# A two-layer mixture-of-experts block with attention: a written order for the first part, a late residual bias, loads held for the first gather, and token rows added in DRAM by the DMA

## The chip, the cores and the metric

The kernel runs on one core of one Trainium2 chip, in one launch. The metric is device time in microseconds (us), the median of several runs; lower is better.

## The reference

The model width D is 1024. There are T = 512 latent tokens x and 256 context tokens s. Everything is float32. The kernel computes two blocks; the change touches the first, which has two layers. The second (two more attentions and convolutional feed-forward layers) follows unchanged and is left out here.

```python
for i in range(2):                                  # first block
    sh1, sc1, g1, sh2, sc2, g2 = adaln(c, w_mod[i], b_mod[i])     # silu(c) @ w_mod + b_mod, 6 x D
    a = rmsnorm(x, norm1_g[i]) * (1 + sc1) + sh1
    if i == 0:   y = pool_mixer(a)                  # the same on the context, with its own c
    else:        y = attn_mixer(a, a_ctx)           # 16 query heads, 4 key heads, keys of x and s
    x = x + g1 * y
    x = x + g2 * hier_moe(rmsnorm(x, norm2_g[i]) * (1 + sc2) + sh2)
    # layer 0 does both lines for the context s too; layer 1 only reads it

def pool_mixer(h):                 # 4 groups of 256 channels, windows of 2, 4, 8, 16 tokens
    p = [window_mean(h_g, w) - h_g for g, w in groups]
    return (einsum(p, w_pool) + b_pool) * ls

def hier_moe(h):                   # 16 experts in 4 groups: best group, then top 2 in it
    gates = ...                    # one row of 16 per token, two of them not zero
    a, b = h @ w_gate[e], h @ w_up[e]               # 1024 x 256 for each expert e
    return sum_e (silu(a) * b * gates[e]) @ w_down[e]
```

## The kernel before

**Layout.** Channels lie on partitions in 8 chunks of 128, tokens along the free axis: x is 8 x (128 x 512), the context xc is 8 x (128 x 256). Matrix products with large weights are made from three float32-round products: `split_w` (L285 to 296) casts a weight tile to its high part (L294, ScalarE) and subtracts it for the low part (L295, DVE or GpSimd); `mm3` (L353 to 355) adds the three products. Weights come by `load_raw` (L303 to 320): each load is 512 KB, all are issued on SyncE's queue and keep their written order. Their slots are a ring of 6 tiles of the pool `raw` and two for each larger tile given to `ring`; a load waits until the slot is read out. A load can be given a *hold*: it then waits for a named DMA, and since the queue is in order all later loads wait with it.

**Order.** A planner at build time orders each engine's instructions by priority (written order) and readiness, so written order and engine order differ unless an edge is added by hand (`issue_after`, `add_manual_dep`).

**Layer 0, first part (L1085 to 1155).** w_mod has 12 blocks of 2 MB for each layer, in the order 0, 2, 1, 3, 4, 5, 8, 9, 6, 7, 10, 11. A block is `adaln_mm` (four loads, 16 matmuls at L380, a copy by ScalarE at L385) and `adaln_end` (four transposes, two small DVE operations). In between stand, for the latent rows (r = 0) and the context (r = 1) and four channel groups g: `pool_pre` (normalise, L479 and L481), `pool_win` (window sums by scan, L495 to 507) and `pool_back` (the 256 x 256 group product L521, the residual bias by ScalarE at L518, gate and residual add by DVE at L523). Then the MoE's entry: `moe_chunk` (ScalarE scales a chunk at L587 and squares it at L589; the matmuls of the router and of the sum of squares at L594), `moe_shift` (the shift's part of the logits, and the shift as broadcast rows `b2r`, copied at L615), `moe_close` (evacuation L622, transposes, logits L627, 1/rms with ScalarE's square root L192, L630, L631) and `moe_tr` (transposes of a token block and, on DVE at L648, times 1/rms plus shift; L649 writes the rows to `h2d` in DRAM, by GpSimd's queue in layer 0 and by ScalarE's in layer 1).

**Routing and experts (`moe_run`).** DVE turns the logits into lists of token numbers per expert (to L780). GpSimd gathers an expert's rows from `h2d` with an indirect DMA (L834), 128 rows in layer 0 and 96 in layer 1; TensorE transposes them (`rows_t`), then come gate/up and down products, and ScalarE's queue writes results to `yd` (L899). At the end `fetch` gathers two rows of `yd` for each token. `Stream` issues expert weights (four loads gate/up and two loads down for each expert) some experts ahead. In layer 0 it also carries two blocks of layer 1's w_mod, at the places "a" and "b" ahead of the routing; each of these calls `more(1)` twice, which issues the next expert weights.

**Layer 1** has the latent rows alone: `moe_shift` stands ahead of the output product wo (`gemm_8`), whose chunks call `moe_chunk` as they come; then five tiles are given to the ring, `moe_close`, `moe_tr` and `moe_run` follow.

Of the kernel before, what the change touches and what calls it, by code (L numbers as in the profile page):

```python
# [63 lines left out]
def build(tc, A, out, stop=None, dbg=None):  # L64
# [98 lines left out]
    def vc(name, i=0, n=1):  # L163
        o = _VEC[name] + i
        return vec[:, o : o + n]

# [155 lines left out]
    class Stream:  # L322
# [50 lines left out]
    def adaln_mm(l, nb, st=None, got=None):  # L373
        ps = PS()
        if not st and got is None:
            got = adaln_load(l, nb)
        for u in range(2):
            raw = st.take(("ad", l, nb, u)) if st else got[u]
            for kk in range(4):
                mm(ps[32 * kk : 32 * kk + 32, :], cs[:, 4 * u + kk, :], raw[kk // 2][:, kk % 2 * 512 : kk % 2 * 512 + 512],  # L380
                   start=(u == 0), stop=(u == 1), tile_position=(0, 32 * kk))
            if st:
                st.more(1)
        adps[l, nb] = t2()
        S.copy(adps[l, nb], ps)  # L385
# [126 lines left out]
    def pool_back(r, g):  # L512
        xr, n, _ = rows[r]
        ps_p = pooled.pop((r, g))
        g_, b_ = gl[r, g // 2]
        for f in range(2):
            c = 2 * g + f
# [5 lines left out]
            V.scalar_tensor_tensor(xr[:, c, :], ps[:, :n], g_[:, c % 4 : c % 4 + 1], xr[:, c, :], op0=ALU.mult, op1=ALU.add)  # L523
# [29 lines left out]
    def moe_start(l, segs, cap):  # L553
# [5 lines left out]
        for xr, n, r in segs:  # L559
            q = K()  # L560
            q.xr, q.n, q.r, q.nb, q.tb0, q.psl, q.seen, q.due = xr, n, r, n // 128, st.ntb, None, 0, []
            st.ntb += q.nb
            st.segs.append(q)
# [15 lines left out]
    def moe_chunk(st, i, c):  # L579
# [7 lines left out]
        S.activation(hch(q, c), q.xr[:, c, :], AF.Copy, scale=q.a2[:, c : c + 1])  # L587
        sq = t2()
        S.activation(sq[:, : q.n], q.xr[:, c, :], AF.Square)  # L589
        q.due += [(st.wr[:, c, :], hch(q, c)), (e20, sq[:, : q.n])]  # L590
        if len(q.due) == 4:

            for k, (w, v) in enumerate(q.due):
                mm(q.psl[32 * k : 32 * k + 32, : q.n], w, v, start=q.seen == 0, stop=q.seen == 3, tile_position=(0, 32 * k))  # L594
            q.due = []
            q.seen += 1

    def moe_shift(st, i):
# [11 lines left out]
        q.b2r = half("b2")  # L610
        for h_ in range(2):
            pt = PS()
            for c in range(4):
                transpose(pt[:, c * 128 : c * 128 + 128], b2[:, 4 * h_ + c : 4 * h_ + c + 1].to_broadcast([128, 128]))
            S.copy(q.b2r[:, 512 * h_ : 512 * h_ + 512], pt)  # L615

    def moe_close(st, i):
# [4 lines left out]
        S.copy(ev[:, :n], q.psl[:, :n])  # L622
# [5 lines left out]
        q.rs = rstd_from(lg[:, :, 20], 1.0 / D, [128, nb], f"n2_{q.r}")  # L628
        lg = lg[:, :, 0:20]
# [3 lines left out]
        def tr(b):  # L633
# [10 lines left out]
            def second():  # L644
                ht = half("ht")
                for h_, pt in enumerate(pts):
                    hs_ = slice(512 * h_, 512 * h_ + 512)
                    V.scalar_tensor_tensor(ht[:, hs_], pt, q.rs[:, b : b + 1], q.b2r[:, hs_], op0=ALU.mult, op1=ALU.add)  # L648
                (G if len(st.segs) > 1 else S).dma_start(st.h2d[(q.tb0 + b) * 128 : (q.tb0 + b) * 128 + 128, :], ht)  # L649
# [3 lines left out]
        st.trs += [tr(b) for b in range(nb)]  # L653

# [13 lines left out]
    def moe_run(st, wst):  # L668
# [121 lines left out]

        def late():


            gd = gsm([128, N, 4], tag="gd")
            V.tensor_tensor(gd, gl_, bc(gm.rearrange("p (n o) -> p n o", o=1), [128, N, 4]), op=ALU.subtract)
# [4 lines left out]
            v1, v2 = (gsm([128, N], tag=f"v{j}") for j in range(2))  # L800
            for v_, va in ((v1, v1a), (v2, v2a)):
                V.tensor_tensor(va, va, goh, op=ALU.mult)
                V.reduce_sum(v_, va, axis=AX.X)
            ed = gsm([128, N], tag="ed")
            V.tensor_tensor(ed, v2, v1, op=ALU.subtract)
# [34 lines left out]
        def gather(e):  # L840
            xg[e] = half("xg")
            gather_rows(xg[e][0:cap, :], idx[0:cap, e : e + 1])
# [240 lines left out]


    mst = moe_start(0, rows, 128)  # L1085
    sss = [stats(0)]
    adaln_block(0, 0)
    rb[0] = bcast(sss[0].compact("n1_0"), T)
    adaln_block(0, 2)
    a1[0, 0] = half_cols(0, 0)  # L1090
    pool_pre(0, 0)
    adaln_mm(0, 1)
    pool_win(0, 0)
    pool_pre(0, 1)
    adaln_end(0, 1)
    adaln_mm(0, 3)
    pool_win(0, 1)
    adaln_end(0, 3)
    a1[0, 1] = half_cols(0, 1)
    nc.sync.dma_start(poolw, A["poolw"])  # L1100
    adaln_mm(0, 4)
    pool_pre(0, 2)
    adaln_end(0, 4)
    nc.sync.dma_start(xc, A["ctxT"])
    pool_win(0, 2)
    gl[0, 0] = half_gate(0, 0)
    pool_back(0, 0)
    adaln_mm(0, 5)
    pool_pre(0, 3)
    pool_back(0, 1)  # L1110
    adaln_end(0, 5)
    pool_win(0, 3)
    sss.append(stats(1))
    gl[0, 1] = half_gate(0, 1)
    for h_ in range(2):
        a1[1, h_] = half_cols(1, h_)
        gl[1, h_] = half_gate(1, h_)
    pool_back(0, 2)
    adaln_mm(0, 8)
    rb[1] = bcast(sss[1].compact("n1_1"), TC)  # L1120
    pool_pre(1, 0)
    adaln_end(0, 8)
    pool_back(0, 3)
    pool_win(1, 0)
    adaln_mm(0, 9)
    pool_pre(1, 1)
    adaln_end(0, 9)
    pool_win(1, 1)
    for c in range(4):
        moe_chunk(mst, 0, c)  # L1130
    pool_back(1, 0)
    adaln_mm(0, 6)
    pool_pre(1, 2)
    for c in range(4, 8):
        moe_chunk(mst, 0, c)
    adaln_end(0, 6)
    pool_win(1, 2)
    pool_back(1, 1)
    adaln_mm(0, 7)
    pool_pre(1, 3)  # L1140
    adaln_end(0, 7)
    pool_win(1, 3)
    moe_shift(mst, 0)
    moe_shift(mst, 1)
    pool_back(1, 2)
    moe_close(mst, 0)
    pool_back(1, 3)
    for c in range(4):
        moe_chunk(mst, 1, c)
    moe_tr(mst, 4)  # L1150
    for c in range(4, 8):
        moe_chunk(mst, 1, c)
    adaln_block(0, 10)
    moe_close(mst, 1)
    adaln_block(0, 11)
# [657 lines left out]
    moe_shift(mst, 0)  # L1813
    g1 = shift(1, 2, 0)
# [27 lines left out]
    ring.extend(s8() for _ in range(5))  # L1842
# [676 lines left out]
```

## Time and profile before

| | |
|---|---|
| time, median of 3 runs (lowest, highest) | 2222.83 us (2222.02, 2226.96) |
| the profiled execution: its own time, its span | 2218.79 us, 2217.0 us |
| mean granted TensorE clock, share of full speed | 0.973 |
| busy: PE, DVE, ACT, POOL | 93%, 64%, 50%, 23% |
| moved by DMA | 323.43 MB, mean 146 GB/s |

PE is TensorE, DVE VectorE, ACT ScalarE, POOL GpSimd and SP SyncE. PEld is TensorE's weight load; a name with q (SPq, ACTq) is an engine's issuing of DMAs. Times in the rows are from the start of the span. The first part of layer 0 and its MoE lie at 0 to 316 us, layer 1's at 316 to 873 us.

### The profile page before, as it was taken

Reading aid. Unit: us, or ns where it says so; the run is one execution under the profiler, and the core shown is the slowest. Engines: PE = TensorE matmul, PEld = TensorE weight load, DVE = VectorE, ACT = ScalarE, POOL = GpSimd, SP = SyncE. Lnnn points to the kernel's source line nnn. Section 1 sums busy time; section 2 is a strip of 40 time slices with the busy share of each in tenths; the row PEclk is TensorE's granted clock in tenths of the full one; section 3 lists DMA queues with packets and bytes.
Section 4 is the critical chain, followed back from the end, with each engine's and each line's share of the span. In section 5 each row is a group of like instructions: output and inputs, shape, how many; then the busy total and the mean of one; then the engine's idle time right before and its main releaser. Section 6 shows DMA issues by size and latency. Waiting matters only on the chain.

```text
span 2217.0 us, 32294 instructions
## 1 busy us (share of the span) xinstructions
PE 2067.5 (93%) x12233; PEld 1683.7 (76%) x12233; DVE 1418.8 (64%) x2304; ACT 1102.1 (50%) x1967; POOL 509.6 (23%) x513
## 2 busy tenths in 40 slices
PE   6869998999994999999999999999999999999997
PEld 1348767788863767776698888999878888888997
DVE  4579878778726987367847666626363568565633
ACT  3648864488833886344434434324253455343422
POOL 1011021477201212245423101014100024101011
PEclk9889999999997999999999999999999999999998
DMA  9699973124606996321113333332322212333321
GB/s 376 260 351 398 417 282 101 50 77 137 217 21 219 369 391 211 99 77 48 58 52 102 94 100 91 98 93 68 97 86 86 67 48 89 101 96 96 96 77 39
DMA packets 94207, 323.43 MB, mean 146 GB/s; under 512 B 11537, under 2 KB 17184, under 8 KB 93536
## 3 DMA queue, kind: packets, MB, share of 16 engines
q1 hardware_dynamic: 76480, 274.76, 36.0%
q0 software_dynamic: 7968, 28.32, 3.6%
q10 hardware_dynamic: 9600, 18.26, 2.2%
q8 instruction: 97, 1.59, 0.3%
q14 instruction: 62, 0.51, 0.1%
HBM read 301.02 MB, written 20.27 MB: 145 GB/s over the span
## 4 chain that ended last, share of the span: by engine, by line
PE 65%; DVE 7%; DMA 4%; POOL 3%; ACT 3%; issue 3%; ACTq 0%; DVEq 0%; POOLq 0%; SPq 0%
PE ps L353 19%; PE ps L355 18%; PE ps L354 18%; PE ps L177 3%; DMA s<-in_mgu_dram 1%; PE ps L1722 1%; DVE lo L295 1%; POOL raw L1762 1%; PE ps L2103 1%; PE ps L2254 1%; DVE s L1939 1%; ACT hi L294 1%; DMA raw<-in_mdn_dram 1%; PE ps L2059 1%; DVE s L1931 1%
## 5 line engine op out<-in xcount | busy, mean ns | idle before, releaser
L353 PE MATMUL ps<-s,hi 128*128 128x512 f32 (+1 forms) x1440 | 513.5, 358 | 4.3 <-DVE s L1931 3.2
L354 PE MATMUL ps<-s,hi 128*128 128x512 f32 (+1 forms) x1440 | 505.6, 351 | 3.0 <-DVE s L1939 1.8
L355 PE MATMUL ps<-s,lo 128*128 128x512 f32 (+1 forms) x1440 | 507.4, 353 | 0.0
L294 ACT CAST hi<-raw 128x1024 fp32r<-128x1024 f32 x284 | 294.0, 1047 | 419.2 <-PE ps L354 334.2
L295 DVE TENSOR_TENSOR lo<-raw,hi 128x1024 fp32r<-128x1024 f32 x232 | 288.2, 1256 | 277.5 <-ACT hi L294 277.3
L295 POOL TENSOR_TENSOR lo<-raw,hi 128x1024 fp32r<-128x1024 f32 x52 | 125.4, 2411 | 892.1 <-ACT hi L294 892.1
L353 PEld LDWEIGHTS ps<-s,hi 128*128 128x128 f32 x1440 | 270.5, 188 | 45.7 <-issue 8.0
L354 PEld LDWEIGHTS ps<-s,hi 128*128 128x128 f32 x1440 | 271.3, 188 | 41.4 <-DVE s L1939 2.4
L355 PEld LDWEIGHTS ps<-s,lo 128*128 128x128 f32 x1440 | 271.1, 188 | 41.1 <-issue 0.5
L353 PE MATMUL ps<-hi,s 128*128 128x512 f32 (+1 forms) x528 | 216.8, 412 | 4.6 <-ACT hi L294 2.0
L354 PE MATMUL ps<-lo,s 128*128 128x512 f32 (+1 forms) x528 | 211.9, 401 | 2.6 <-DVE lo L295 2.6
L355 PE MATMUL ps<-hi,s 128*128 128x512 f32 (+1 forms) x528 | 211.3, 401 | 2.5 <-DVE s L1839 2.5
L355 PE MATMUL ps<-t2r,lo 128*128 128x256 f32 (+1 forms) x640 | 188.2, 294 | 0.0
L354 PE MATMUL ps<-t2r,hi 128*128 128x256 f32 (+1 forms) x640 | 187.8, 293 | 0.0
L353 PE MATMUL ps<-t2r,hi 128*128 128x256 f32 (+1 forms) x640 | 187.8, 293 | 0.0
L353 PEld LDWEIGHTS ps<-hi,s 128*128 128x128 f32 (+1 forms) x528 | 105.3, 199 | 30.1 <-ACT hi L294 4.4
L355 PEld LDWEIGHTS ps<-hi,s 128*128 128x128 f32 (+1 forms) x528 | 105.2, 199 | 29.0 <-DVE s L1839 4.1
L354 PEld LDWEIGHTS ps<-lo,s 128*128 128x128 f32 (+1 forms) x528 | 105.9, 201 | 25.7 <-DVE lo L295 3.1
L353 PEld LDWEIGHTS ps<-t2r,hi 128*128 128x128 f32 x640 | 121.2, 189 | 5.2 <-issue 2.5
L354 PEld LDWEIGHTS ps<-t2r,hi 128*128 128x128 f32 x640 | 121.1, 189 | 5.3 <-issue 2.5
L355 PEld LDWEIGHTS ps<-t2r,lo 128*128 128x128 f32 x640 | 120.8, 189 | 5.2 <-issue 2.5
L295 DVE TENSOR_TENSOR lo<-s,hi 128x1024 fp32r<-128x1024 f32 x98 | 114.8, 1217 | 5.2 <-ACT hi L294 4.7
(371 smaller groups left out, 3667.2 us busy)
## 6 DMA issues: line engine op xcount, KB each, us to landing
raw<-in_up_dram SPq DMA_DIRECT2D x88, 512.0 KB
s<-in_mgu_dram SPq DMA_DIRECT2D x64, 512.0 KB
raw<-in_mgu_dram SPq DMA_DIRECT2D x44, 512.0 KB
raw<-in_down_dram SPq DMA_DIRECT2D x44, 512.0 KB
raw<-in_dilqkv_dram SPq DMA_DIRECT2D x36, 512.0 KB
s<-in_mdn_dram SPq DMA_DIRECT2D x34, 512.0 KB
raw<-in_wmodT_dram SPq DMA_DIRECT2D x32, 512.0 KB
s<-in_wmod_dram SPq DMA_DIRECT2D x30, 512.0 KB
```

Source lines behind the costliest of these rows:

```text
L177: return PE.transpose(dst, src, ident if idt is None else idt)
L294: S.copy(hi, raw)
L295: eng.tensor_tensor(lo, raw, hi, op=ALU.subtract)
L353: mm(ps, ahi, bhi, start=start, stop=False)
L354: mm(ps, ahi, blo, start=False, stop=False)
L355: return mm(ps, alo, bhi, start=False, stop=stop)
L1722: mm(po_[c][o : o + 64, qb * 128 : qb * 128 + 128], vview[:, kc, c // 2 * 64 : c // 2 * 64 + 64], PTs[h_][:, kc * 128 : kc * 128 + 128], s ...
L1762: G.tensor_tensor(w, w, crow, op=ALU.mult)
L1931: V.tensor_tensor(mv, mv, bc(self.rb[:, None, 0:256], [128, 2, 256]), op=ALU.mult)
L1939: V.scalar_tensor_tensor(self.h.lo(c)[:, ts], x[:, c, ts], g_, self.h.hi(c)[:, ts], op0=ALU.mult, op1=ALU.subtract)
L2059: mm(pz[:, o : o + n], qq, kk, start=True, stop=True)
L2103: mm(po[64 * hh : 64 * hh + 64, kb * 128 : 512], vt, at[:, o : o + n], start=(kb == 0), stop=(kb == 3), tile_position=(0, 64 * hh))
```

## The change

- **A written order.** `in_order` links the instructions of TensorE, ScalarE and DVE in the whole first part, each to the one before it on its engine, so that they run as written. The part is written anew: the first four blocks' loads ahead, each later block's loads after the matmuls of an earlier one; `pool_back` is cut into `back_mm` and `back_add`; context squares are summed by matmuls (`sum_stats`); context chunks alternate with the `moe_tr` of one token block; blocks 10 and 11 come after everything else.
- **The bias late.** The 16 operations at L518 leave `pool_back`. `moe_chunk` takes the bias into its scale and its square; `back_bias` adds it to the residual after the last `moe_close`.
- **Loads held.** The places "a" and "b" no longer issue expert loads. These 8 loads follow the first gather in layer 0, and are held until it has landed. Six small DVE operations of the gate weights are moved ahead of the first weight splits.
- **Layer 1's rows.** The shift rows are written to `h2d` by ScalarE's queue well ahead. `moe_tr` then needs only a scaled copy by ScalarE in place of L648, and GpSimd's queue issues a DMA that adds the rows to those in DRAM. The square-root table is loaded right after the evacuation, and the ring gets its five tiles ahead of wo.

```diff
+    @contextlib.contextmanager
+    def in_order():
+        cur = nc.cur_bb.bb.instructions
+        known = {id(i) for i in cur}
+        yield
+        prev = {}
+        for i in cur:
+            if id(i) in known or i.engine not in (V.engine, S.engine, PE.engine):
+                continue
+            if i.engine in prev:
+                tc.add_manual_dep(i, prev[i.engine].name, mybir.DependencyInfo(
+                    mybir.DependencyClass.NoSync, mybir.DependencyReason.DATA), reason="in order")
+            prev[i.engine] = i
...
-                adaln_mm(*b, self)
+                adaln_mm(*b, self, more=k not in ("a", "b"))
...
-            S.activation(xr[:, c, :], xr[:, c, :], AF.Identity, bias=b_[:, c % 4 : c % 4 + 1])
...
+    def back_bias(r):
+        xr, n, _ = rows[r]
+        for c in range(NCH):
+            S.activation(xr[:, c, :], xr[:, c, :], AF.Identity, bias=gl[r, c // 4][1][:, c % 4 : c % 4 + 1])
...
+            S.activation(hch(q, c), q.xr[:, c, :], AF.Identity, scale=q.a2[:, c : c + 1], bias=q.a2b[:, c : c + 1])
+            S.activation(sq[:, : q.n], q.xr[:, c, :], AF.Square, bias=bias[c // 4][:, c % 4 : c % 4 + 1])
...
+        evac = S.copy(ev[:, :n], q.psl[:, :n])
+        if len(st.segs) == 1:
+            sqrt_table(evac)
...
+                    if q.there:
+                        st.s_last = S.activation(ht[:, hs_], pt, AF.Copy, scale=q.rs[:, b : b + 1])
+                    else:
+                        V.scalar_tensor_tensor(ht[:, hs_], pt, q.rs[:, b : b + 1], q.b2r[:, hs_], op0=ALU.mult, op1=ALU.add)
+                if q.there:
+                    G.dma_start(to, ht, accum_op=ALU.add)
+                else:
+                    G.dma_start(to, ht)
...
+            for b in range(q.nb):
+                S.dma_start(st.h2d[(q.tb0 + b) * 128 : (q.tb0 + b) * 128 + 128, :], q.b2r)
...
-        for e in range(3):
+        first = gather(0)
+        with tc.issue_after(gated.ins):
+            firsts = late_first()
+        if wst.ads:
+            hold[:] = [first]
+            wst.more(2 * sum(len(v) for v in wst.ads.values()))
+        for e in range(1, 3):
             gather(e)
         wst.side("c")
         if not wgu:
-            with tc.issue_after(gated.ins):
+            with tc.issue_after(firsts.ins), tc.issue_after(st.s_last.ins):
                 moe_weights(st, wst, 0, V)
...
+        ad(5, 7)
...
+        ad(8, 10)
...
+        ad(9, 11)
+        back_add(1, 0)
+        chunks(0, 0)
+        pool_win(1, 3)
+        back_add(1, 1)
+        back_mm(1, 2)
+        ad(6)
+        chunks(0, 1)
+        back_mm(1, 3)
+        back_add(1, 2)
+        ad(7)
+        back_add(1, 3)
+        moe_shift(mst, 0)
+        moe_shift(mst, 1)
+        chunks(0, 2)
+        moe_shift_rows(mst, 0)
+        chunks(0, 3)
+        moe_close(mst, 0)
+        chunks(1, 0)
+        moe_tr(mst, 1)
...
+        chunks(1, 3)
+        moe_tr(mst, 1)
+        moe_close(mst, 1)
+        moe_shift_rows(mst, 1)
+        for r in range(2):
+            back_bias(r)
+    ad(10)
+    ad(11)
...
+    moe_shift_rows(mst, 0, there=True)
+    ring.extend(s8() for _ in range(5))
...
-    ring.extend(s8() for _ in range(5))
```

## Rows read from the trace of the kernel before

**Rows 1.** Windows: busy time of each engine in seven stretches.
```profile
40.00:97.00 57.00, 49.72 (x206) 17.57 (x202) 31.79 (x76) 28.55 (x57) 2.96 (x15) 0.90 0.86 336
97.00:118.00 21.00, 16.45 (x125) 12.91 (x124) 12.77 (x32) 10.69 (x27) 2.38 (x4) 0.84 0.38 143
137.00:146.00 9.00, 0.61 (x3) 0.64 (x4) 5.19 (x13) 0.00 (x0) 5.60 (x4) 0.50 1.03 416
180.00:283.00 103.00, 101.34 (x486) 82.36 (x485) 93.55 (x108) 89.50 (x128) 11.30 (x10) 1.00 1.02 415
620.00:670.00 50.00, 49.39 (x190) 30.57 (x189) 10.24 (x13) 15.29 (x23) 2.40 (x1) 1.00 0.04 11
690.00:700.00 10.00, 1.78 (x16) 1.58 (x16) 5.81 (x13) 0.25 (x1) 5.51 (x4) 0.50 1.03 380
785.00:825.00 40.00, 37.69 (x184) 26.30 (x184) 34.40 (x41) 32.97 (x50) 9.19 (x4) 1.00 1.03 389
```

**Rows 2.** Timeline of ACT, 90 to 122 us: start, duration, idle before and releaser.
```profile
95.87 0.59 ACT L385 COPY t<-ps 128x512 f32<-128x512 f32 x1 [2.95 <-PE ps L380]
...
117.02 0.58 ACT L385 COPY t<-ps 128x512 f32<-128x512 f32 x1 [5.94 <-PE ps L380]
117.50 0.38 ACT L622 COPY t<-ps 128x256 f32<-128x256 f32 x1
```

**Rows 3.** Timeline of DVE, 100 to 124 us: the last operation on the logits.
```profile
120.36 0.20 DVE L631 TENSOR_TENSOR g<-g,g 128x40 f32<-128x40 f32 x1
```

**Rows 4.** Groups by line and shape, 0 to 137 us: busy, mean ns, idle before.
```profile
L518 ACT ACTIVATE x<-x,sm 128x512 f32<-128x512 f32 x8 | 5.2, 711 | 4.3 <-DVE sm L450 4.3
L518 ACT ACTIVATE xc<-xc,sm 128x256 f32<-128x256 f32 x8 | 3.8, 495 | 0.0
```

**Rows 5.** Waits of SP's queue, 50 to 160 us: in total, times, longest.
```profile
SPq L314 <- PE ps L380: 47.9, 11, 19.8
```

**Rows 6.** Timeline, 134 to 150 us: the first gathers of layer 0.
```profile
136.72 0.16 DVE L780 CAST g<-ps 128x14 int32<-128x14 f32 x1
136.80 4.62 DVE L295 TENSOR_TENSOR lo<-raw,hi 128x1024 fp32r<-128x1024 f32 x4
137.09 1.82 POOL L834 DMA_INDIRECT s<-h2d,g  x1 [10.35 <-DVE g L780]
...
141.43 0.94 POOL L834 DMA_INDIRECT s<-h2d,g  x1 [0.30 <-issue]
...
145.39 1.94 PE L177 MATMUL ps<-ident,s 128*128 128x128 f32 x8 [8.81 <-DMA s<-h2d,g]
```

**Rows 7.** Timeline, 296 to 320 us: the last gathers of the latent rows in layer 0.
```profile
307.00 1.87 POOL L834 DMA_INDIRECT s<-yd,g  x1 [0.30 <-issue]
...
313.63 1.29 DVE L930 SCALAR_TENSOR_TENSOR s<-s,g 128x1024 f32<-128x1024 f32 x1 [1.77 <-DMA s<-yd,g]
313.65 3.19 SPq L314 DMA_DIRECT2D raw<-in_wmod_dram  x6
```

**Rows 8.** Waits of TensorE, 165 to 300 us.
```profile
PE ps L353 <- ACT hi L294: 1.6, 3, 0.7
```

**Rows 9.** Timeline, 670 to 706 us: layer 1 from its last logits to its first rows.
```profile
673.40 1.28 ACT L192 ACT_TABLE_LOAD   x1
...
676.07 0.75 DVE L648 SCALAR_TENSOR_TENSOR s<-ps,sm,s 128x512 f32<-128x512 f32 x1
...
691.48 1.78 POOL L834 DMA_INDIRECT s<-h2d,g  x1 [53.51 <-DVE g L780]
...
698.84 1.51 PE L177 MATMUL ps<-ident,s 96*128 96x96 f32 x8 [7.85 <-DMA s<-h2d,g]
```

**Rows 10.** Groups by line and shape, 670 to 700 us.
```profile
L648 DVE SCALAR_TENSOR_TENSOR s<-ps,sm,s 128x512 f32<-128x512 f32 x8 | 5.8, 740 | 0.0
```

**Rows 11.** The chain that ended last, 600 to 720 us: start, duration, what.
```profile
678.97 2.67 DMA h2d<-s
...
693.57 10.53 DMA s<-h2d,g
```

**Rows 12.** Waits of SP's queue, 590 to 700 us.
```profile
SPq L314 <- DMA h2d<-s: 55.2, 4, 48.8
```

More of the change, by code (lines that the diff above doesn't have):

```diff
@@ L371, in adaln_load, with adaln_mm @@
         return [load_raw(A["wmod"][l, nb, :, 2048 * u : 2048 * u + 2048]) for u in range(2)]
-    def adaln_mm(l, nb, st=None, got=None):
+    def adaln_mm(l, nb, st=None, got=None, more=True):
         ps = PS()
@@ L381, in adaln_mm @@
                    start=(u == 0), stop=(u == 1), tile_position=(0, 32 * kk))
-            if st:
+            if st and more:
                 st.more(1)
@@ L560, in moe_start @@
             q = K()
[L561 removed]
+            q.xr, q.n, q.r, q.nb, q.tb0, q.psl, q.seen, q.due, q.there = xr, n, r, n // 128, st.ntb, None, 0, [], False
             st.ntb += q.nb
@@ L577, in hch, with moe_chunk @@
         return q.hts[c // per][:, (c % per) * q.n : (c % per) * q.n + q.n]
-    def moe_chunk(st, i, c):
+    def moe_chunk(st, i, c, bias=None):
         q = st.segs[i]
@@ L609, in moe_shift @@
         V.tensor_tensor(q.cst[:, 0, :], pc[:, 0:20], rbias[:, st.l, :], op=ALU.add)
[L610 to L615, printed above, removed]
     def moe_close(st, i):
@@ L1104, in build @@
[L1104 to L1155, printed above, removed]
+    got = {}
+    def ad_load(nb):
+        got[nb] = adaln_load(0, nb)
+    def ad(nb, nxt=None):
+        adaln_mm(0, nb, got=got.pop(nb))
+        if nxt is not None:
+            ad_load(nxt)
+        adaln_end(0, nb)
+    def chunks(i, j):
+        for c in (2 * j, 2 * j + 1):
+            moe_chunk(mst, i, c, bias=[gl[i, h_][1] for h_ in range(2)])
@@ new lines, in build @@
+    mst = moe_start(0, rows, 128)
+    with in_order():
+        for nb in (0, 2, 1, 3):
+            ad_load(nb)
+        nc.sync.dma_start(poolw, A["poolw"])
+        ss0 = stats(0)
+        ad(0, 4)
+        nc.sync.dma_start(xc, A["ctxT"])
+        rb[0] = bcast(ss0.compact("n1_0"), T)
+        ad(2, 5)
+        a1[0, 0] = half_cols(0, 0)
+        pool_pre(0, 0)
+        pool_pre(0, 1)
+        pool_win(0, 0)
+        pool_win(0, 1)
+        ad(1, 8)
+        ad(3, 9)
+        a1[0, 1] = half_cols(0, 1)
+        pool_pre(0, 2)
+        back_mm(0, 0)
+        pool_pre(0, 3)
+        pool_win(0, 2)
+        ad(4, 6)
+        gl[0, 0] = half_gate(0, 0)
+        back_mm(0, 1)
+        for h_ in range(2):
+            a1[1, h_] = half_cols(1, h_)
+        ss1 = sum_stats(1)
+        pool_win(0, 3)
+        back_add(0, 0)
+        back_add(0, 1)
+        rb[1] = bcast(rstd_from(ss1, 1.0 / D, [128, 2], "n1_1"), TC)
+        pool_pre(1, 0)
+        ad(5, 7)
+        gl[0, 1] = half_gate(0, 1)
+        for h_ in range(2):
+            gl[1, h_] = half_gate(1, h_)
+        back_mm(0, 2)
+        back_mm(0, 3)
+        pool_pre(1, 1)
+        pool_win(1, 0)
+        back_add(0, 2)
+        back_add(0, 3)
+        pool_pre(1, 2)
+        pool_win(1, 1)
+        ad(8, 10)
+        back_mm(1, 0)
+        pool_pre(1, 3)
+        back_mm(1, 1)
+        pool_win(1, 2)
+        ad(9, 11)
[18 more added lines that the diff above has]
+        moe_tr(mst, 1)
+        chunks(1, 1)
+        moe_tr(mst, 1)
+        chunks(1, 2)
+        moe_tr(mst, 1)
+        chunks(1, 3)
+        moe_tr(mst, 1)
+        moe_close(mst, 1)
+        moe_shift_rows(mst, 1)
+        for r in range(2):
+            back_bias(r)
```

92 lines of the change are left out of this document (54 added, 38 removed).

## The prediction, made before the changed kernel was run

> **What bounds the kernel now.** I read the windows first, then the timelines at their borders, then the waits and the chain. The windows [rows 1] show that the two layers are made of stretches with different limits. In the experts of layer 0 (180 to 283 us) PE is busy 101.34 of 103 us while the DMA engines are full too (1.02): the two are in balance, and PE waited for data only 1.6 us between 165 and 300 us [rows 8]. In layer 1's experts the DMA engines are full again and PE loses 2.3 of 40 us. What is not full lies ahead of the experts. In 40 to 118 us PE is busy 66.2 of 78 us, DVE 44.6, ACT 39.2, and the DMA engines are down to 0.38 at the end: the order sets the time there, not an engine. From 137 to 146 us and from 690 to 700 us PE does almost nothing and waits for the first gather, with the DMA engines at 1.03. So only three spans can give time: the first part to the last logits at 120.56 us [rows 3], the gather of layer 0 (137.09 to 145.39 us [rows 6]), and layer 1 from its table load at 673.40 to its first rows at 698.84 us [rows 9]. All that comes after 873 us stays as it is, and shifts by what these give.
>
> **The first part in written order.** Removed from ahead of the routing are the 16 bias operations, 5.2 + 3.8 = 9.0 us of ACT [rows 4]; they come back after the last logits as `back_bias`. There ACT has little to do until the rows arrive, DVE's routing (16.2 us from 120.56 to 136.72 [rows 3, 6]) covers them, so they cost nothing; with the cover gone they would cost 9.0 us. ACT isn't full ahead of the routing either (39.2 of 78 us), so the removal gives little by itself.
>
> What the order changes can be read at three places. First, the second evacuation of logits, at 117.50 us, stood on ACT behind the copy of block 10, which ACT had awaited for 5.94 us [rows 2]. In the new order block 10 comes after it: up to 5.9 us gained. Second, two of the four steps of latent chunks now stand after block 7's copy instead of before it, and the transposes and shift rows stay between; that gives back about the same. I walked the written list, starting each instruction when its engine and operands are ready, with the durations of the trace. It puts the copy of block 7 at about 93.5 us (95.87 before [rows 2]) and the last logits at 120 to 122 us (120.56). Third, loads: SP waited 47.9 us for matmuls of w_mod, once 19.8 [rows 5]; blocks 10 and 11 are now read later still, at about 120 us, and expert 0's weights queue behind their slots. The idle DMA time ahead of 118 us, 0.62 of 21 us, is therefore not recovered. Sum of the first part: 0. The bounds are below: all of PE's idle time in 40 to 118 us, 11.8 us, gained; or the overlap partly lost, up to 24 us.
>
> **The held loads.** Eight loads of 512 KB go behind the first gather. At 416 GB/s [rows 1] they are 4.19 MB / 0.416 = 10.1 us of DMA time. The first gather took 8.30 us from issue to the first transpose [rows 6], with the engines full. The nearest gather without loads beside it is the last one of the latent rows, 307.00 to 313.63 = 6.63 us; SP's next loads start behind it [rows 7]. That one still shared the engines with other gathers, so the gain is 1.7 us or more. An upper end is the issue alone: GpSimd took 1.82 us while DVE made weight splits, and 0.94 after them [rows 6]; the new order delays the splits by six small DVE operations, which may give 0.9, and a transfer alone may give 1.26 more (512 KB at 416 GB/s). I take -2.5 (ends -1.7 and -4).
>
> The price is the lead of the DMA over PE. The eight loads cost 10.1 us of DMA time; the stretch in which the engines would have idled for them is the gather itself. Since both are full in the experts [rows 1], what is missing at the start isn't made up. Before, PE waited only 1.6 us in the experts [rows 8], so a part of the lead was spare, but how much no row shows. I take +2, ends 0 and +10. The Trainium skill ("DMA: Bandwidth & Descriptors", "Queues, rings and completion order") says that queues are served in turn by an arbiter, packet by packet. By that rule a gather beside one load queue loses only its share, 1.3 us for 512 KB at 416 GB/s; the sum would then be -1.3 instead of -2.5, and no row before shows which. Layer 0 together: 0 - 2.5 + 2 = -0.5 us.
>
> **Layer 1's rows.** (a) The table load, 1.28 us at 673.40 [rows 9], stands in the chain between the logits and the root, behind weight casts; put right after the evacuation it is hidden by the transposes: -1.3 to -2, I take -1.8. (b) The eight DVE operations at L648, 5.8 us [rows 10], stand among the routing's and leave DVE. Part of them filled gaps between dependent small operations, so I count -4.2 of the 5.8 (ends -3 and -5.8). ACT gets eight copies of 128 x 512 instead; at L385's 0.58 us [rows 2] that is 4.6 us, on an engine that has nothing urgent. The gather's issue, 691.48 us [rows 9], moves to 691.5 - 1.8 - 4.2 = 685.5. (c) The rows must be in DRAM by then. L648 began at 676.07 [rows 9], the copies may begin 1.8 us sooner, at 674.3, and take 4.6 us, so the last ends at about 679; a plain write took 2.67 us from issue to landing [rows 11], so the last one would land at about 682. No row shows an adding DMA. Below, it costs as a plain one; reading and writing twice the bytes, 5.3 us, lands at 684.5: both in time. Above, four in strict succession at 5.3 us, the first issued at 675.5, end at 696.7. The row that it is nearest to is the plain write, so I take no cost up to +1.5. (d) SP's queue waited 48.8 us for the landing of a row write [rows 12], and the DMA engines moved nothing from 620 to 670 us [rows 1]. When the wait ended, loads, row writes and gathers met, at 1.03 from 690 to 700 us; the second gather took 10.53 us [rows 11]. With the ring extended ahead of wo, those loads find their slots earlier, and the gathers are nearly alone: at the 6.63 us of [rows 7] the first lands at 692.1, the second, issued 2.1 us later as before [rows 9, 11], at 694.2 instead of 704.1. PE's first product stands behind both, so it comes 9.9 us earlier. The loads moved into the hole also give the DMA the lead that an earlier start of the experts needs (10 us at 389 GB/s are 7.4 loads). I take -8.5 (ends -3 and -12): 1.4 us are left for (c) and for loads that still meet the gather.
>
> The Trainium skill ("SBUF — State Buffer", "Who interferes with whom") speaks against (c): a DMA that GpSimd issues has its descriptors written in software, and these starve while DVE holds the port that both share; it advises ScalarE's or SyncE's queue, which is where the writes came from. The trace agrees in direction: issues of 1.82 us beside DVE's splits, 0.94 behind them [rows 6]. By it, four issues at 1.9 us instead of 0.94 under the routing would end at about 683.5 us, the last rows would land at 686 to 689, and layer 1 would give 5 to 8 us instead of 8.5.
>
> **The sum.** -0.5 - 8.5 = -9 us. Against the profiled execution, 2218.79 us (a span of 2217.0 and 1.8 around it), that is 2209.8. The median of the runs, 2222.83, is 4.0 above that execution and all three runs are above it; I forecast the median: 2222.8 - 9 = 2213.8, say 2214.
>
> **Rivals.** *The order pays in full.* PE's idle time in 40 to 118 us goes, 11.8 us [rows 1], because no planner lets a late block stand ahead of urgent work, and the 5.94 us hold of [rows 2] is proof of such. Against it: the walk. Time: 2214 - 12 = 2202. *The order stalls* (the other side): the mechanism is that in 40 to 97 us PE's 49.7 and DVE's 31.8 us [rows 1] now overlap by 24.5 us because the planner takes what is ready; in a fixed order a `back_add` that waits for its product holds the next group's window sums, and these the next product. If all overlap went, +24.5; from 0.55 of it, 13.4 us, the kernel is slower by over 0.2%. For it: blocks' loads come when they come, and the list was laid out for one set of arrivals. At three quarters: 2214 + 18 = 2232. *The adding DMA is slow.* If four run in succession, rows are ready at 696.7 or later instead of 685.5; at 5.3 us each layer 1's gain is gone: 2222; at twice that, 2232. For it: adds to the same tensor must be kept in order by somebody. *The lead is missing in full:* +10 instead of +2 in layer 0: 2222.
>
> **Chances and range.** The forecast 0.46, the order that pays 0.15, the order that stalls 0.17, the slow adding DMA 0.14 (0.04 of it beyond the change of sign), the missing lead 0.08. 0.2%, 4.4 us, is about what a measurement here can tell from no change; that is 2218.4 to 2227.2. Faster: 0.43 of the forecast's 0.46 and 0.15, 0.58. Same: 0.03 + 0.10 + 0.08 = 0.21. Slower: 0.17 + 0.04 = 0.21. The forecast's own range is 2209 to 2219 (layer 0 from -3 to +4, layer 1 from -6 to -11); the range that leaves out 2 in 10 reaches from the order that pays, 2200, to just short of the stalls, 2231.
>
> **What would show it.** In the changed kernel: the last operation on the logits (the one that L631 is now) at 120 to 122 us; no load beside the first gather of layer 0, which takes 6 to 6.6 us; PE waits for weights (lines of `mm3`) of some 2 us more in the experts; in layer 1 no table load between logits and root, DVE without row operations, the gather's issue about 6 us and the first product about 10 us earlier relative to the evacuation; the rows' DMAs landed before the gather is issued. Wrong would make it: an ACT or DVE idle of several us with a releaser of the pool mixer, GpSimd waiting for the adding DMAs ahead of the gather, or experts that wait for DMA.

## The result, and the profile after

The changed kernel takes 2248.34 us in the median of four runs (2245.05 to 2253.02); the kernel before, run beside it, 2223.82 us (2222.02 to 2226.96, four runs). The ratio is 1.011, with a 95% interval of 1.0088 to 1.0132: slower by 24.5 us, where 9 us less were forecast (2214, range 2200 to 2231). The profiled execution took 2248.62 us over a span of 2246.9, 29.9 us more than the one before. That is 5.4 more than 24.5, mostly because the profiled execution of the kernel before (2218.79) was 5.0 us faster than its median.

Cut at marks that both traces have, the 29.9 us are these. Times are those of the profiled executions, from the start of the span.

| stretch | before | after | difference |
|---|---|---|---|
| start to the last operation on layer 0's logits (its end) | 120.6 | 130.7 | +10.1 |
| to the issue of the first gather | 16.5 | 29.4 | +12.9 |
| to the first expert product | 12.4 | 8.7 | -3.7 |
| to the first residual operation behind the experts | 166.0 | 167.7 | +1.7 |
| to the evacuation of layer 1's logits | 355.4 | 366.0 | +10.6 |
| to the first expert product of layer 1 | 34.5 | 30.9 | -3.6 |
| to the end | 1511.6 | 1513.5 | +1.9 |

Two of these were forecast about as they came (the held gather, the experts' lead), one came at less than half its size (layer 1), two of +23 us together were forecast as nothing, and one lies for the most part in code that the change leaves as it was.

Windows of the changed kernel; columns as in [rows 1]:

```profile
40.00:101.00 61.00, 50.54 (x230) 23.02 (x229) 34.23 (x86) 18.28 (x36) 0.71 (x12) 0.86 0.80 312
101.00:131.00 30.00, 21.34 (x126) 10.93 (x126) 12.26 (x40) 16.73 (x34) 2.37 (x4) 0.77 0.33 131
180.00:283.00 103.00, 101.61 (x488) 82.65 (x487) 93.46 (x109) 88.60 (x127) 13.38 (x12) 1.00 1.03 416
650.00:700.00 50.00, 50.00 (x195) 31.74 (x193) 12.59 (x16) 14.92 (x23) 2.43 (x1) 1.00 0.49 187
```

From 101 us on the written order runs no engine at its limit: PE is busy 21.3 of 30 us, ACT 16.7, the DMA engines a third, and the granted clock is 0.77 of full speed. The experts are as full as before, and the hole of 0.04 in the DMA ahead of layer 1 [rows 1] is half filled.

ACT's timeline in two stretches, 92 to 131 us and 126 to 192 us (L401 is L385 of before, L717 is L615, L552 the bias that was L518):

```profile
100.24 0.58 ACT L401 COPY t<-ps 128x512 f32<-128x512 f32 x1 [5.03 <-PE ps L396]
100.72 0.81 ACT L635 ACTIVATE s<-x,sm,sm 128x512 f32<-128x512 f32 x1
101.44 0.71 ACT L636 ACTIVATE t<-x,sm 128x512 f32<-128x512 f32 x1
...
108.71 0.58 ACT L717 COPY s<-ps 128x512 f32<-128x512 f32 x1 [5.24 <-PE ps L193]
...
130.19 5.01 ACT L552 ACTIVATE x<-x,sm 128x512 f32<-128x512 f32 x8
135.09 3.29 ACT L552 ACTIVATE xc<-xc,sm 128x256 f32<-128x256 f32 x8
138.28 0.57 ACT L401 COPY t<-ps 128x512 f32<-128x512 f32 x1
```

Read the last three lines first. Block 10's product was done at 130.7 us, but its copy stands behind the 16 biases, 8.1 us, and begins at 138.28. What that holds shows on PE (timeline, 112 to 175 us) and DVE (129 to 172 us):

```profile
138.90 1.11 PE L193 MATMUL ps<-ident,t 128*128 128x128 f32 x4 [8.20 <-ACT t L401]
...
149.80 0.21 PE L785 MATMUL ps<-g,tri 128*128 128x96 bf16 x1
...
165.53 3.65 PE L193 MATMUL ps<-ident,s 128*128 128x128 f32 x16 [5.94 <-DMA s<-h2d,g]
```

```profile
130.47 0.20 DVE L678 TENSOR_TENSOR g<-g,g 128x40 f32<-128x40 f32 x1
...
134.25 0.26 DVE L778 TENSOR_TENSOR g<-g 128x96 bf16<-128x96 f32 x1
...
150.41 0.26 DVE L810 TENSOR_TENSOR g<-ps,ebase 128x96 f32<-128x96 f32 x1
```

PE waits 8.20 us for block 10's copy, then does block 10's transposes, block 11, the transposes of the last token rows and the first of layer 1's two blocks, and only then, at 149.80 us, the routing's first product (L785), whose operand DVE had ready at 134.5. That is 19.1 us behind the logits. In the kernel before it came 6.2 us behind them (PE, 112 to 150 us, where L716 is L785):

```profile
126.72 0.22 PE L716 MATMUL ps<-g,tri 128*128 128x96 bf16 x1
```

In the changed kernel DVE's routing goes on at 150.41. The last operation on the logits (L678, L631 of [rows 3]) is itself 10.1 us late.

POOL, 120 to 172 us: the first gather leaves at 160.10 us, and PE has its rows 5.43 us later, against 8.30 before [rows 6]:

```profile
160.10 1.02 POOL L907 DMA_INDIRECT s<-h2d,g  x1 [11.01 <-DVE g L868]
```

Layer 1's attention, where nothing was edited, DVE and POOL from 541 to 557 us, and the same addition in the trace before (DVE, 515 to 530 us):

```profile
544.83 10.53 DVE L1836 TENSOR_TENSOR sm<-sm 128x8 f32<-128x8 f32 x1
```

```profile
539.92 7.12 POOL L1868 TENSOR_TENSOR raw<-raw,xc 128x1024 f32<-128x1024 f32 x3
546.93 0.56 POOL L1717 CAST s<-s 128x384 fp32r<-128x384 f32 x1
547.40 1.05 POOL L1718 TENSOR_TENSOR s<-ktok,s 128x384 fp32r<-128x384 f32 x1
548.35 6.99 POOL L1868 TENSOR_TENSOR raw<-raw,xc 128x1024 f32<-128x1024 f32 x3
```

```profile
520.44 2.11 DVE L1730 TENSOR_TENSOR sm<-sm 128x8 f32<-128x8 f32 x1
```

An addition of 8 columns takes 10.53 us and ends at 555.36, when GpSimd's run of operations ends (548.35 + 6.99 = 555.34). The same addition took 2.11 us in the trace before, so 8.4 of the 10.6 us of that stretch stand in this line.

Layer 1's entry: POOL from 700 to 736 us, one line each of ACT (the evacuation) and DVE (the last operation on the lists) in the same stretch, and two steps of the chain:

```profile
707.35 2.04 POOL L701 DMA_DIRECT2D h2d<-s  x2 [37.78 <-ACT s L697]
709.64 0.86 POOL L701 DMA_DIRECT2D h2d<-s  x1 [0.25 <-ACT s L697]
710.79 0.86 POOL L701 DMA_DIRECT2D h2d<-s  x1 [0.29 <-ACT s L697]
723.38 0.99 POOL L907 DMA_INDIRECT s<-h2d,g  x1 [11.73 <-DMA h2d<-s]
```

```profile
702.52 0.58 ACT L666 COPY t<-ps 128x512 f32<-128x512 f32 x1 [1.14 <-PE ps L644]
```

```profile
716.06 0.16 DVE L849 CAST g<-ps 128x12 int32<-128x12 f32 x1
```

```profile
710.79 11.74 DMA h2d<-s
723.38 7.18 DMA s<-h2d,g
```

The lists were ready at 716.22, 13.7 us behind the evacuation (702.52) where they were 20.4 behind it before: table and row operations left the chain, 6.7 us, as forecast (6.0). But the fourth adding DMA landed 11.74 us after its issue, and the gather waited for it until 723.38: 7.2 us given back. The gather then took 7.18 us.

### The profile page after: what moved, and what is told of

Same layout as the page of the kernel before. It is cut to its first block, busy times and chain, and to the rows that moved or that the text cites. A ratio compares the mean times of both kernels' runs of the same rounds, so it can differ in the third digit from the quotient of the medians.

```text
span 2246.9 us, 32355 instructions
## 1 busy us (share of the span) xinstructions
PE 2075.7 (92%) x12257; PEld 1689.1 (75%) x12257; DVE 1422.7 (63%) x2297; ACT 1111.1 (49%) x1976; POOL 512.7 (23%) x514
## 4 chain that ended last, share of the span: by engine, by line
PE 65%; DVE 7%; DMA 4%; POOL 3%; ACT 2%; issue 2%; DVEq 0%; POOLq 0%; ACTq 0%; SPq 0%
PE ps L369 18%; PE ps L370 18%; PE ps L371 18%; PE ps L193 4%; PE ps L1828 1%; DMA s<-in_mgu_dram 1%; POOL raw L1868 1%; DVE lo L311 1%; PE ps L2361 1%; PE ps L2210 1%; PE ps L2409 1%; DVE s L2046 1%; PE ps L2166 1%; DMA s<-in_mdn_dram 1%; DVE sm L1836 1%
## 5 line engine op out<-in xcount | busy, mean ns | idle before, releaser
L370 PEld LDWEIGHTS ps<-t2r,hi 128*128 128x128 f32 x640 | 120.6, 189 | 5.0 <-issue 2.5
## 6 DMA issues: line engine op xcount, KB each, us to landing
s<-in_mdn_dram SPq DMA_DIRECT2D x34, 512.0 KB, 10.5
s<-in_wmod_dram SPq DMA_DIRECT2D x30, 512.0 KB, 10.2
```

The source lines that it names most:

```text
L370: mm(ps, ahi, blo, start=False, stop=False)
```

## The experiments

Line numbers in rows are those of each kernel. The marks of all runs, from one profile of each; "longest DVE" is the longest duration among the attention's eight additions and the eight copies behind them:

| run | time against before (95%) | logits | gather | first product | last result out | longest DVE | layer 1: gather, product behind evacuation |
|---|---|---|---|---|---|---|---|
| before | 1 | 120.6 | 137.1 | 149.5 | 293.4 | 2.2 | 20.6, 34.5 |
| after | 1.011 (1.0088, 1.0132) | 130.7 | 160.1 | 168.8 | 314.2 | 10.5 | 20.9, 30.9 |
| e1 | 1.0089 (1.0073, 1.0106) | 132.2 | 153.0 | 161.7 | 308.8 | 10.5 | 19.2, 30.3 |
| e2 | 1.0006 (0.9993, 1.0019) | 121.1 | 141.5 | 150.2 | 296.2 | 2.5 | 19.5, 30.8 |
| e3 | 0.9978 (0.9966, 0.999) | 120.5 | 137.0 | 149.5 | 294.5 | 2.4 | 21.0, 30.1 |
| e4 | 0.9993 (0.9977, 1.0009) | 117.3 | 133.8 | 146.2 | 294.3 | 2.2 | 19.3, 33.0 |
| e5 | 1.0118 (1.0083, 1.0152) | 127.7 | 157.1 | 165.9 | 312.4 | 10.2 | 18.8, 30.4 |
| e6 | 1.0036 (1.0017, 1.0055) | 117.4 | 144.3 | 152.9 | 301.3 | 10.5 | 20.9, 30.9 |
| e8 | 0.9966 (0.9946, 0.9987) | 120.8 | 137.3 | 145.7 | 291.8 | 2.5 | 19.2, 29.5 |
| e9 | 0.9966 (0.9945, 0.9987) | 118.8 | 135.3 | 147.7 | 292.6 | 10.4 | 13.9, 27.2 |
| e10 | 0.9935 (0.9909, 0.9961) | 117.9 | 134.4 | 142.9 | 289.2 | 0.7 | 20.6, 30.7 |
| e11 | 0.9964 (0.9951, 0.9977) | 118.8 | 135.4 | 147.7 | 292.8 | 0.7 | 20.6, 34.0 |
| e12 | 0.995 (0.9929, 0.997) | 115.0 | 134.7 | 143.3 | 289.8 | 0.7 | 18.8, 30.2 |
| e13 | 1.0052 (1.0032, 1.0072) | 131.2 | 160.7 | 169.3 | 315.6 | 0.7 | 20.1, 30.9 |

With the same first part the logits end anywhere from 117.3 to 121.1 us, so marks of layer 0 that are less than 4 us apart tell nothing by themselves.

**e1, the biases later.** From the list `back_bias` goes behind the last w_mod block multiplied ahead of the gather.

```diff
-        for r in range(2):
-            back_bias(r)
...
+        if wst.ads:
+            with tc.issue_after(adcp[1, 1].ins):
+                for r in range(2):
+                    back_bias(r)
         first = gather(0)
```

> The changed kernel with the 16 late bias operations ordered on ScalarE behind the copy of the last w_mod block that is multiplied ahead of the gather, in place of behind the last 1/rms of the first part. Theory A (the biases stand on ScalarE ahead of block 10's copy; TensorE's queue waits for that copy, and the routing's first product is queued behind it): block 10's copy ends about 7 to 8 us sooner, the routing's first product and the first gather too, the kernel takes about 2240 us. Rival B (the routing's product is held by the blocks' own products and loads, whatever ScalarE does): the gather stays where it is, 2248 us.

2243.08 us. Block 10's copy ran right behind its product, and the routing's product came 9.7 us behind the logits in place of 19.1 (ACT's timeline, 130 to 156 us, and PE's, 130 to 146 us):

```profile
132.34 0.59 ACT L401 COPY t<-ps 128x512 f32<-128x512 f32 x1 [0.55 <-PE ps L396]
...
144.45 1.05 ACT L310 CAST hi<-raw 128x1024 fp32r<-128x1024 f32 x1 [3.19 <-DMA h2d<-pw]
...
145.88 5.02 ACT L552 ACTIVATE x<-x,sm 128x512 f32<-128x512 f32 x8
```

```profile
141.81 0.21 PE L785 MATMUL ps<-g,tri 128*128 128x96 bf16 x1
```

Theory A holds: from logits to gather 29.4 became 20.8 us. The gather and the first product came 7.1 us sooner; the last result 5.4 and the end of the span 4.7 us. By the medians it is 5.3 us, but the intervals of the two ratios overlap, so that the shift is shown by the queues and not by the total. Of the 4.3 us that remain over the 16.5 of before, 3.5 lie ahead of the routing's product (9.7 us behind the logits, 6.2 before): blocks 10 and 11 now stand there. The rest goes with a cast of ACT that waits 3.19 us for token rows to leave a tile; e2 below shows the same wait.

**e6, no order edges.** The same list, ordered by the planner.

```diff
-            if i.engine in prev:
+            if False:
                 tc.add_manual_dep(i, prev[i.engine].name, ...)
```

> The changed kernel without the edges of the written order: the same instructions written in the same list, ordered by the planner. Theory A (the fixed order itself costs the 10 us up to the last logits): last logits at 120 to 124 us in place of 130, total 8 us less or more, 2240 us. Rival B (what the list contains and where the biases and the shift rows stand costs, whoever orders it): last logits at 128 us or later, 2246 us or more.

2235.37 us, 0.0074 of the ratio or some 16 us better than the change. DVE's timeline, 114 to 118 us:

```profile
117.15 0.20 DVE L678 TENSOR_TENSOR g<-g,g 128x40 f32<-128x40 f32 x1
```

Theory A, and by more than it said: the edges alone cost 13.3 us at the logits, and the same list without them is at the level of the old first part (117.3 to 121.1). The four profiles with edges (after, e1, e5, e13) have the logits at 127.7 to 132.2 us, the two of the list without them (e6, e12) at 117.4 and 115.0.

**e2, e3, e4 and e8, parts alone.** e2 is the changed kernel with the old first part; e3 is the kernel before with layer 1's part; e4 is the kernel before with two pieces of that part alone, the table load and the ring's tiles; e8 is e2 with the token rows of layer 0 in tiles of their own.

```diff
# e4: of layer 1's part only these two
+        if len(st.segs) == 1:
+            sqrt_table(evac)
+    ring.extend(s8() for _ in range(5))          # ahead of wo
# e8, against e2
-                ht = wide() if len(st.segs) > 1 else half("ht")
+                ht = half("ht")
```

> The changed kernel with the first part of the kernel before (planner's order, bias ahead of the product, context squares by the vector engines), the held loads and layer 1's rows as changed. Theory A (the written list itself puts the last logits at 130 us, and the bias the gather at 161 us): last logits at 120 to 121 us, first gather at 136 to 138 us, 2216 to 2222 us, where up to 8 us depend on how long one small DVE addition in layer 1's attention waits for GpSimd. Rival B (the held loads cost the lead of the DMA, and layer 1's rows cost): 2226 us or more though the first part is as before.

> The kernel before with layer 1's part of the change alone: shift rows written early, scaled copies on ScalarE, the adding DMA, the table load and the ring's tiles ahead of wo. Theory A (adding DMAs land one after the other, 2.5 to 4.4 us each): the first gather waits for the fourth to land, about 15 us after the first is issued; from the evacuation of the logits to the first gate product 30 to 31 us, where it was 34.5; total 2219 to 2222 us. Rival B (they are slow only beside the weight loads of the changed kernel's timing): first product 26 us or less behind the evacuation, 2214 us.

> As the last, but with rows made by DVE and written plainly by ScalarE's queue as before; only the table load and the ring's tiles are moved. Theory A (what gained in layer 1 is the loads in the hole and the table, not the adding DMA): first gather issued about 2 us sooner than before against the evacuation, second gather 7 us long in place of 10.5, first gate product 5 to 6 us sooner, 2217 us. Rival B (rows off DVE are what gains): first product 2 us sooner, 2221 us.

> The run with the old first part and the held loads, with the token rows of layer 0 in tiles of their own again, in place of tiles shared with the high parts of weights. Theory A (a weight's cast waited 5.7 us for a row write to leave such a tile, and the routing behind it on ScalarE, TensorE and DVE): first gather at 137 us in place of 141.5; the experts are bound by the DMA so that at most half of it reaches the end: 2221 us. Rival B (the wait is for something else): gather at 141 us, 2224 us.

e2: 2224.23 us, between the two theories. The first part's 10 us are gone with the old list, but the gather left at 141.5 and not at 137. The waits of 121 to 152 us say why:

```profile
ACT hi L310 <- DMA h2d<-pw: 5.7, 1, 5.7
```

A weight's cast writes a tile from which token rows were still on their way to DRAM; ACT, PE and DVE stood behind it in turn. The sharing is part of the change (`wide()` in place of `half("ht")` in `moe_tr`), but neither its description nor the prediction has it. In the changed kernel itself the same wait is 0.89 us, as its casts come late anyway. e8 takes the tile out of that pool: gather at 137.3 us, 2220.05 us. Theory A, and more of it reached the end than half: the last result came 4.4 us sooner. In e8 the first product comes 8.4 us after the gather, in the kernel before 12.4: holding the loads gives 4.0 us there, and the last result is 1.6 us sooner.

e3: 2217.24 us, and the gather behind the evacuation by 21.0 us, the product by 30.1: Theory A at the marks, with a total 2 us below its range. e4: 33.0 and 2221.63 us, where theory A said 29 and 2217; it falls, and the numbers are rival B's. Of the 4.4 us that e3 gains at the product, table and ring alone give 1.5. The other 2.9, with the adding DMA's wait already paid, are not rows off DVE alone: the waits of SP's queue from 590 to 700 us (in total, times, longest), e4 first and then e3, show that the ring's tiles by themselves did not bring the loads forward.

```profile
SPq L314 <- DMA h2d<-s: 71.3, 4, 65.6
```

```profile
SPq L314 <- DMA h2d<-s: 32.8, 3, 30.2
```

In e4 a load waited 65.6 us for a row write, the DMA engines moved nothing from 640 to 670 us, as in the kernel before, and the loads met the gathers. In e3, where the shift rows are written early, the longest such wait is 30.2 us and the hole is partly filled. Which share belongs to the loads and which to DVE no run parts.

**e9, rows not added.** As e3, without `accum_op`: the scaled rows replace the shift rows, and so the kernel leaves the shift out of layer 1's expert inputs.

```diff
-                    G.dma_start(to, ht, accum_op=ALU.add)
+                    G.dma_start(to, ht)
```

> Layer 1's part alone as before, but GpSimd's queue writes the scaled rows plainly over the shift rows in place of adding them: the shift is left out of layer 1's expert inputs. Theory A (the adding itself is slow): the four writes land within 4 us of the last issue, the gather is issued when the lists are ready, 14 us behind the evacuation in place of 21, first product 24 us behind it, 2211 us. Rival B (DMAs of GpSimd's queue are slow because DVE and descriptors in software collide): rows land 10 us after the last issue as when added, 2217 us.

2217.24 us, which was rival B's total and not theory A's 2211. POOL's timeline, 680 to 702 us:

```profile
684.75 0.63 POOL L659 DMA_DIRECT2D h2d<-s  x1 [37.74 <-ACT s L654]
...
688.21 0.53 POOL L659 DMA_DIRECT2D h2d<-s  x1 [0.62 <-ACT s L654]
693.84 1.77 POOL L846 DMA_INDIRECT s<-h2d,g  x1 [5.10 <-DVE g L792]
```

The writes took GpSimd 0.53 to 0.63 us each, beside the routing on DVE, and the gather waited for the lists alone (DVE L792): it left 13.9 us behind the evacuation. So the adding is what is slow, not the queue. The product came 27.2 us behind, not 24: now the gather met four loads and DVE's splits and its issue took 1.77 us. So at the product the adding costs 2.9 us (30.1 less 27.2), and not the 7 that the gather waits; the totals of e3 and e9 can't be told apart.

What the adding takes of the DMA engines is in the views of the DMA queues (packets, MB, share of the 16 engines' time), first the changed kernel from 707 to 723 us, then e9 from 684 to 694 us:

```profile
q0 software_dynamic: 576, 2.10, 74.8%
```

```profile
q0 software_dynamic: 576, 2.10, 52.8%
```

The same 2.10 MB took 12.0 us of all 16 engines when added and 5.3 us when written plainly. Four weight loads ran beside the end of the first and none beside the second.

**e5, e13 and e11, the DVE wait.** e5 makes the addition a reduction in the changed kernel; e13 also the operation behind it; e11 does both in the kernel before.

```diff
-        V.tensor_tensor(rd, den[:, :, :, 0], den[:, :, :, 1], op=ALU.add)
+        V.reduce_sum(rd, den, axis=AX.X)
...
-        V.tensor_copy(rdx.rearrange("p (q h e) -> p q h e", q=4, h=2),
-                      bc(rd.rearrange("p q (h o) -> p q h o", o=1), [128, 4, 2, 64]))
+        V.reduce_sum(rdx.rearrange("p (g e) -> p g e", g=8),
+                     bc(rd.rearrange("p q h -> p (q h)")[:, :, None, None], [128, 8, 64, 1]), axis=AX.X)
```

> The changed kernel with one edit in layer 1's attention: the eight small DVE additions of two softmax partial sums (two operands in SBUF) are made by a DVE reduction over the same pairs (one operand). Theory A (an addition with two SBUF operands waits for GpSimd's long run of multiplications, 10.5 us once and 2.3 once in the changed kernel's trace; an operation with one operand doesn't): all eight take 0.2 to 0.4 us, the logits of layer 1 come 8 to 12 us sooner, 2236 to 2240 us. Rival B (any DVE operation in that place waits): some of the eight still take 2 to 10 us, 2246 us or more.

> The changed kernel with the two attention operations as reductions. Theory A (a part of the loss is the DVE wait of 10.5 us, which the kernel before has in some of its executions only): 2236 to 2241 us with a spread under 8 us. Rival B (the wait has nothing to do with the loss, or moves on to another operation as in the run with one of the two changed): 2246 us or more.

> The kernel before with the same two operations of layer 1's attention in the form of reductions, and nothing else. Theory A: its times lose the group 8 us above the other, and the three waits of 2.1 to 2.2 us: median 2216 to 2219 us. Rival B: no change, 2223 to 2226 us.

e5 gained nothing (2250.4 us). All eight reductions took 0.16 to 0.17 us; the wait moved one operation on, to the copy that spreads the reciprocal (DVE, 540 to 553 us):

```profile
541.26 0.16 DVE L1836 TENSOR_REDUCE sm<-sm 128x8 f32<-128x16 f32 x1
541.76 10.23 DVE L1839 COPY t<-sm 128x512 f32<-128x512 f32 x1
```

So neither theory as put, though the total is rival B's: not any operation waits, and not only those with two operands. With both as reductions no wait is left (e13, each of the two lines as one group; the three numbers are the shortest, the median and the longest duration in ns, then the first and last start):

```profile
L1836 DVE TENSOR_REDUCE sm<-sm x8: 159/165/171, 480.4 to 623.2; 128x8 f32<-128x16 f32 x8
L1839 DVE TENSOR_REDUCE t<-sm x8: 680/686/686, 480.9 to 623.6; 128x512 f32<-128x512 f32 x8
```

e13 takes 2235.51 us and e11 2217.72 us, both in theory A's terms, except that e13's times still spread over 15.5 us: the change loses 0.0058 of its ratio, 13 us, and the kernel before 0.0036, 8 us (6 by the medians). The longer wait can come without the change: e9, whose first part is that of before, had one of 10.4 us in its profile; before, e2, e3, e4 and e8 had 2.2 to 2.5. But all four profiles with the written list in which one of these operations can still wait (after, e1, e5, e6) have the long form, so that the change may make it likelier; one profile of each kernel can't settle it. The order of each engine's instructions in the attention is the same in the changed kernel and in e2. What decides between 2 and 10 us in an execution wasn't found.

**e10 and e12, what is left when the losses are out.** e10 is e8 with the two reductions. e12 keeps the written list, without edges, with the biases of e1, the tiles of e8 and the reductions.

> The run with the old first part, held loads, own tiles for the rows and layer 1's rows as changed, and with two small DVE operations of layer 1's attention in another form: the sum of the partial sums as a reduction, and the spread of its reciprocal over 512 columns as a reduction over single elements in place of a copy. Theory A (only DVE operations on SBUF of two operands, or fast copies, wait for GpSimd's run; a reduction doesn't): none of the 16 takes over 1 us; the two groups of times 8 us apart become one; median 2213 us. Rival B (what DVE runs next there waits in their place): a wait of 2 to 10 us stands at another DVE operation, 2220 us.

> The changed kernel with all that was found put right, and with its written list kept: no order edges, the late biases behind the last w_mod block ahead of the gather, rows in tiles of their own, the two attention operations as reductions. Theory A (edges, biases, tiles and the DVE wait made the loss; the list itself is worth 3 us): last logits at 117 us, gather at 133 to 135 us, 2210 to 2214 us. Rival B (the experts of layer 0 are bound by loads that the list issues late): gather as early, but the last expert no sooner than in the run with the old first part, 2216 us or more.

e10: 2212.3 us, e12: 2213.35 us, both as theory A had the totals. Both beat the kernel before by more than their intervals. More than half of that is the reductions, which are no part of the change: against e11, which has them too, e10 is 5.4 us faster by the medians, and six of its seven times lie below the fastest of e11's twelve. So held loads and layer 1's part are worth some 5 us of the 9 forecast. The list gives earlier logits (115.0 us) and loses it on the way to the gather (19.7 us, against 16.5 in e10), because blocks 10 and 11 stand in between. The 3 us that theory A gave it did not show.

## Why the prediction was wrong, step by step

**The step that failed first: "they cost nothing".** The late biases were said to lie under DVE's routing. DVE's 16 us cover them, but ACT was not idle there: block 10's copy stands behind them, PE's queue behind the copy, the routing's first product behind that. The price without cover was given as 9.0 us; e1 moved the biases and got 8.6 us between logits and gather. The other 4.3 of the 12.9 us are mostly blocks 10 and 11 behind the logits (3.5 at the routing's product). The prediction had itself noted that blocks 10 and 11 now come last, and did not follow that step through the queues.

**The sum of the first part, 0.** It was +10.1 at the logits, and 13.3 by the edges alone (e6). The walk put block 7's copy at 93.5 us; it came at 100.2. Behind it the walk had about 27 us, the trace has 30: ACT stood 5.24 us for the shift rows' transposes, which PE does behind products that wait for DVE, and the chunk operations with a bias take 0.81 and 0.71 us where the ones without took 0.71 and 0.62. The rival of the stalling order had the sign, with 24.5 us as its end and 13.4 us as the point where it decides. Its mechanism was right in kind, and its place only in part: of the 10.1 us, 4.4 lie ahead of block 7's copy (95.87 us before) and 5.7 behind it.

**The held loads.** -2.5 was forecast (-1.7 to -4), the trace gave -2.9 up to the first transpose and -3.7 up to the first product (e8: -4.0). The Trainium skill ("DMA: Bandwidth & Descriptors", "Queues, rings and completion order") has an arbiter serve the queues in turn, from which the prediction had worked out an estimate of -1.3; the measurement is above that. The lead cost +1.5 up to the last result (2 forecast).

**Layer 1.** -8.5 was forecast, -3.6 measured at the first product. The terms (a) and (b) held, 6.7 us against 6.0. The term (c), no cost up to 1.5 us, is one that was mis-sized: the adding DMA made the gather wait 7.2 us, as the rival "the adding DMA is slow" had it, though not to its full price. The fourth landed 15.2 us behind the first issue, where (c) had 21.2 as its upper end and a plain write as its nearest row. At the product that is 2.9 us of the 4.9 missing (e3 against e9); e9, without the adding, stands at -7.3 there (27.2 against 34.5), with a gather that meets loads. The gathers came out as said in (d), at 7.2 us instead of 6.63, but not for its reason alone: the ring's tiles by themselves don't bring the loads forward (e4). The Trainium skill's warning ("SBUF — State Buffer", "Who interferes with whom"), that a DMA of GpSimd's queue starves under DVE, led the prediction to 5 to 8 us and so was nearer by its number; e9 shows that its reason was not the one at work, as plain writes of the same queue were issued in 0.53 to 0.63 us beside DVE.

**What no step named.** The DVE wait in the attention: 8.4 us of the profile's 29.9, about 5 of the median's 24.5 (13 less 8, e13 and e11). It was in the trace before as well, at 2.1 to 2.2 us three times, and wasn't read. The trace before had the short form, and its execution was among the fastest of its kernel.

So +10.1 + 12.9 - 3.7 + 1.7 + 8.4 - 3.6 are 25.8 of the 29.9 us. The other 2.2 in the attention are there with the waits gone too (351.9 us in e13 against 349.6 in e11), and the 1.9 behind layer 1's first product are less than the profiles differ among themselves in that stretch (1510.6 to 1516.4 us); both stay open.

## What to carry to other kernels

When work is moved to a place where its engine looks idle, list what that engine's queue holds there, and follow each item to the next queue: here 8 us of ACT work that nobody waited for stood ahead of a half-microsecond copy, and through it held TensorE and then DVE. A written order must beat a planner stage by stage: the same list without the edges gave the 13 us back. And before an experiment is read by its total, look for a wait in untouched code that comes long or short from one execution to the next; taking it out was worth 0.36% to the kernel before.

## What the runs showed of the hardware

A DVE operation can wait through a whole run of GpSimd's operations, not only one: 10.53 us for an addition of 8 columns, through the one that ran when it began and five more, and 10.23 us for a copy of 512 columns in e5, while reductions of the same data took 0.16 and 0.69 us. The Trainium skill ("SBUF — State Buffer", "Who interferes with whom") says that DVE operations with two SBUF inputs, and copies in the fast modes that use two ports, contend with GpSimd for a shared pair of ports, and that reductions on this chip never do. The three forms agree with that; the ports themselves no row shows.

An adding DMA to DRAM is costly in a way that a plain one is not: four of 512 KB, issued from 707.35 to 710.79 us, landed up to 722.5 and took 12.0 us of all DMA engines, where plain writes of the same rows took 5.3 us (e9).
